# A decoder layer on one core: roots on ScalarE, gain vectors by products, own buffers for the memory's weights, low halves on GpSimd

## The chip, the cores and the metric

The kernel runs on one core of one Trainium2 chip. The metric is the device time of one execution in microseconds (us), less is better. Within a core TensorE multiplies matrices (profile: PE, its weight loads PEld), VectorE (DVE) and ScalarE (ACT) work on tiles, GpSimd (POOL) does the same with other means, and SyncE (SP) here issues nearly all transfers between the chip's main memory and the core's SBUF. [...]

## The reference

One layer over 1024 tokens of 1024 channels, with 256 memory tokens, all in float32:

```
h    = rms_norm(x, norm_mix_pre)                 # x * rsqrt(mean(x*x) + 1e-6) * g
q_d, k_d, v_d, u_p, q_m, gates = split(h @ w_in)
y_attn = diff_attention(q_d, k_d, v_d) @ w_attn_branch      # 8 heads, causal, two softmax maps
y_pool = multiscale_pool(u_p) @ w_pool_branch
mem_n  = rms_norm(mem, norm_mem)
k_m, v_m = split(mem_n @ w_mem_kv)                           # 4 heads of 128
y_mem  = softmax(q_m k_m^T / sqrt(128)) v_m @ w_mem_branch
x  = x + rms_norm((sigmoid-gated sum of y_attn, y_pool, y_mem) @ w_out, norm_mix_post)
h2 = rms_norm(x, norm_ffn_pre)
out = x + rms_norm((gelu(g) * v) @ w_down, norm_ffn_post)    # [g|v] = causal conv3(h2 @ w_up)
```

## The kernel before, in words

Each float32 operand of a product is split in two tiles of a shorter float type: `split` (L82) writes the rounded high half on ScalarE (L86) and the difference, the low half, on VectorE (L87). `mm3` (L94) makes a product of three matmuls: high by high (L95), high by low, low by high (L96, L97).

The change touches three places. The first is the stage that opens the kernel. Rows of 128 tokens of the memory (2 tiles) and of x (8 tiles) are normalized by `norm_rows` (L358): a load per tile (`xt`), the sum of squares by ScalarE's Square with an accumulator (L150; of the memory's second tile on VectorE, L146), the inverse root in `rstd_batch` (L140) by an integer guess and three Newton steps on VectorE (`newton`, L156, twelve short instructions with the scaling of the sum), the scaling of the tile by root and gain in one VectorE instruction (L371), and then `transpose_split` (L170): eight transposes of 128x128 on TensorE (L176), and halves of each four. The gains are loaded as vectors broadcast to all partitions (`load_gain`, L165; tiles gm and gp). Between the pairs of tiles stand the memory's weights: four chunks of 128 key columns and four of 256 rows of value columns, each 512 KB, loaded and split by `wsplit` (L330) through the pool `wst`, in which the raw tile, the high and the low half have two buffers each. A key chunk feeds 24 matmuls of 256 columns (`pk`), a value chunk 12 of 512 columns (`pv`). The first query projection (`pq`, 48 matmuls of 512 columns) and its scores (`pss`) follow.

The second place is the output projection: for each of 8 tiles of tokens two norms by `rstd_of` (L107), one over the product in PSUM, one over the new x, with eleven short VectorE instructions each. The third is the end: `norms` (L1438) takes the roots of four result rows at once while the last but one product runs; the last four rows get half of their sum of squares early (`start_row`, L1461), and behind the last products the other half (L1486), the sum, and the root by `rstd_sums` (L122).

All engines run their instructions in order. The order is made by the language's scheduler out of the order of the text and its own estimates; a tile's buffer is waited for by semaphore. Inverse roots in the attention (L1004) use `newton` and are not changed.

## Time and profile before

| | |
|---|---|
| median of 3 runs | 1747.66 us (1745.94 to 1750.28) |
| the profiled execution | 1744.85 us, its span 1742.8 us |
| TensorE busy | 1711.0 us, 98% of the span |
| VectorE, ScalarE, GpSimd busy | 1272.8, 884.7, 45.4 us |
| moved by transfers | 294.95 MB, mean 169 GB/s |

Times in the rows are in us from the start of the span unless marked ns. A row of a timeline tells start, length, engine, line, operation, tile written and tiles read, their shapes, how many instructions were merged, and in brackets how long the engine had been idle and what released it. Matmuls are pipelined: the distance between two starts tells the pace, the length of one holds its way through the array as well. A busy TensorE is not always one at full pace. The state of a wait is inferred from semaphores.

### The profile page before, as it was taken

Reading aid. Unit: us, or ns where it says so; the run is one execution under the profiler, and the core shown is the slowest. Engines: PE = TensorE matmul, PEld = TensorE weight load, DVE = VectorE, ACT = ScalarE, POOL = GpSimd, SP = SyncE. Lnnn points to the kernel's source line nnn. Section 1 sums busy time; section 2 is a strip of 40 time slices with the busy share of each in tenths; the row PEclk is TensorE's granted clock in tenths of the full one; section 3 lists DMA queues with packets and bytes.
Section 4 is the critical chain, followed back from the end, with each engine's and each line's share of the span. In section 5 each row is a group of like instructions: output and inputs, shape, how many; then the busy total and the mean of one; then the engine's idle time right before and its main releaser. Section 6 shows DMA issues by size and latency. Waiting matters only on the chain.

```text
span 1742.8 us, 22648 instructions
## 1 busy us (share of the span) xinstructions
PE 1711.0 (98%) x8138; PEld 1421.4 (82%) x8138; DVE 1272.8 (73%) x2227; ACT 884.7 (51%) x1551; POOL 45.4 (3%) x103
## 2 busy tenths in 40 slices
PE   6999999999999999999999999999999999999997
PEld 5888888888788888888888888888888888888886
DVE  7775875665675568888866567848888888878476
ACT  6434554444544367777744333645555555543452
POOL 0000000000000011111110000000000000000000
PEclk9999999999999999999999999999999999999999
DMA  7784544354784585765557571473433332583343
GB/s 246 253 315 139 170 156 145 123 170 149 247 243 171 179 240 173 186 169 157 152 178 238 181 229 49 155 236 93 124 112 103 121 97 85 205 290 103 109 147 131
DMA packets 232934, 294.95 MB, mean 169 GB/s; under 512 B 15873, under 2 KB 161526, under 8 KB 230134
## 3 DMA queue, kind: packets, MB, share of 16 engines
q1 hardware_dynamic: 229302, 286.13, 51.6%
q0 software_dynamic: 3520, 7.38, 1.2%
q8 instruction: 64, 1.05, 0.2%
q14 instruction: 48, 0.39, 0.1%
HBM read 201.62 MB, written 85.56 MB: 165 GB/s over the span
## 4 chain that ended last, share of the span: by engine, by line
PE 85%; DVE 7%; DMA 4%; ACT 2%; issue 2%; SPq 0%; DVEq 0%; ACTq 0%
PE pa L95 8%; PE pa L97 8%; PE pa L96 8%; PE pb L95 5%; PE pb L97 5%; PE pb L96 5%; PE pss L900 3%; PE poa L956 2%; PE pe L95 2%; PE pe L97 2%; PE pe L96 2%; PE pya L96 2%; PE pya L95 2%; PE pya L97 2%; PE pd L95 2%; PE pd L97 2%
## 5 line engine op out<-in xcount | busy, mean ns | idle before, releaser
L86 ACT ACTIVATE wpage<-s 128x512 fp32r<-128x512 f32 x136 | 85.2, 627 | 106.9 <-PE pb L97 33.7
L87 DVE TENSOR_TENSOR wpage<-s,wpage 128x512 fp32r<-128x512 f32 x136 | 92.5, 687 | 44.8 <-ACT wpage L86 44.8
L1304 DVE SCALAR_TENSOR_TENSOR cvt<-gv,cols,cvt 128x1023 f32<-128x1023 f32 x88 | 112.4, 1277 | 15.6 <-ACT cvt L1300 15.6
L904 DVE CUSTOM_DVE_ANT_0 z<-pss,hbias 128x256 f32<-128x256 f32 (+7 forms) x128 | 94.4, 752 | 25.7 <-PE pss L900 24.6
L909 ACT ACTIVATE z<-z,mx 128x256 f32<-128x256 f32 (+7 forms) x128 | 98.8, 773 | 20.7 <-DVE mx L904 20.5
L95 PE MATMUL pa<-T,wpage 128*128 128x512 f32 x264 | 102.8, 389 | 0.9 <-DVE gv L252 0.9
L96 PE MATMUL pa<-T,wpage 128*128 128x512 f32 x264 | 102.7, 389 | 0.0
L97 PE MATMUL pa<-T,wpage 128*128 128x512 f32 x264 | 102.7, 389 | 0.0
L900 PE MATMUL pss<-ks,q 128*128 128x512 f32 (+5 forms) x384 | 86.5, 349 | 1.4 <-DVE mx L904 1.4
L86 ACT ACTIVATE page<-blk 128x1024 fp32r<-128x1024 f32 (+1 forms) x42 | 41.4, 988 | 85.8 <-PE pe L96 50.6
L87 DVE TENSOR_TENSOR page<-blk,page 128x1024 fp32r<-128x1024 f32 (+1 forms) x42 | 47.4, 1129 | 38.4 <-ACT page L86 38.4
L900 PEld LDWEIGHTS pss<-ks,q 128*128 128x128 f32 x384 | 62.8, 189 | 11.1 <-DVE mx L904 6.2
L86 ACT ACTIVATE wh<-raw 128x1024 fp32r<-128x1024 f32 (+1 forms) x46 | 41.8, 909 | 57.0 <-issue 16.2
L95 PE MATMUL pd<-page 128*128 128x512 f32 x176 | 68.6, 390 | 1.4 <-ACT row L1414 1.4
L96 PE MATMUL pd<-page 128*128 128x512 f32 x176 | 68.5, 389 | 0.0
L97 PE MATMUL pd<-page 128*128 128x512 f32 x176 | 68.5, 389 | 0.0
L95 PE MATMUL pa<-hT,wpage 128*128 128x512 f32 x168 | 65.5, 390 | 0.0
L97 PE MATMUL pa<-hT,wpage 128*128 128x512 f32 x168 | 65.4, 389 | 0.0
L96 PE MATMUL pa<-hT,wpage 128*128 128x512 f32 x168 | 65.4, 389 | 0.0
L956 PEld LDWEIGHTS poa<-aT,v 128*128 128x128 f32 x480 | 60.6, 190 | 3.0 <-ACT srow L976 1.4
L956 PE MATMUL poa<-aT,v 128*128 128x256 f32 (+1 forms) x480 | 62.4, 280 | 0.0
L87 DVE TENSOR_TENSOR wl<-raw,wh 128x1024 fp32r<-128x1024 f32 (+1 forms) x46 | 47.6, 1034 | 18.1 <-ACT wh L86 18.0
(415 smaller groups left out, 5039.1 us busy)
## 6 DMA issues: line engine op xcount, KB each, us to landing
q<-q_d SPq DMA_DIRECT2D x64, 256.0 KB, 5.3
wd<-in_w_down_dram SPq DMA_DIRECT2D x22, 512.0 KB, 5.7
tw_d<-wd SPq DMA_DIRECT2D x11, 1024.0 KB, 4.6
rawv<-in_w_up_dram SPq DMA_DIRECT2D x22, 512.0 KB, 5.8
rawu<-in_w_up_dram SPq DMA_DIRECT2D x22, 512.0 KB, 3.9
ff_d<-cvt SPq DMA_DIRECT2D x22, 512.0 KB, 4.2
blk<-ff_d SPq DMA_DIRECT2D x20, 512.0 KB, 7.2
br<-tw_d SPq DMA_DIRECT2D x20, 512.0 KB, 3.5
```

What stands on the lines that cost most here:

```text
L86: copy = nc.scalar.activation(out=hi, in_=src, func=AF.Copy)
L87: nc.vector.tensor_tensor(out=lo, in0=src, in1=hi.bitcast(F32), op=ALU.subtract)
L95: nc.tensor.matmul(o, ah, bh, start=first, stop=False, skip_group_check=onto)
L96: nc.tensor.matmul(o, ah, bl, start=False, stop=False, skip_group_check=onto)
L97: return nc.tensor.matmul(o, al, bh, start=False, stop=last, skip_group_check=onto)
L900: last["scores"] = nc.tensor.matmul(pss[:, i * H:i * H + m], q[:, j, c, ts], keys, start=(j == 0), stop=(j == 1))
L904: nc.vector.tensor_tensor_reduce(out=halves(z[:, 0:n]), in0=pss.rearrange("p (a m) -> p a m", a=2)[:, 0:parts, 0:m], in1=halves(biases[h][ ...
L909: nc.scalar.activation(out=z[:, 0:n], in_=z[:, 0:n], func=AF.Exp, scale=-1.0, bias=mx[:, c:c + 1], accum_out=sm if c else sums[:, h, t:t + 1])
L956: nc.tensor.matmul(po[:, qs], (vh, vl)[i][:, k, :], w[j][:, ws], start=(n == 0), stop=(n == len(terms) - 1))
L1304: nc.vector.scalar_tensor_tensor(out=cv[:, sh:], in0=u[:, 0:S - sh], scalar=w, in1=cv[:, sh:], op0=ALU.mult, op1=ALU.add)
```

## The change

Inverse roots: `newton`, `rstd_sums` and the two-halves form of `rstd_of` leave the paths named above. ScalarE takes the square root of the mean, VectorE its reciprocal and one Newton step (`rstd_root`, three or four short instructions; one more makes the scaled mean). The second memory tile's squares go from VectorE to ScalarE. The memory's tiles are normalized one by one, x still in pairs. A one-element square root at the start has ScalarE's table loaded; the exponential of the lambda is ordered behind the stage's last root.

Gains: the two vectors are loaded as two rows of one tile, split, and spread over the partitions by eight matmuls with a 2x128 choice of ones and zeros; the scaling reads them from PSUM. Before these matmuls stand 18 transposes of the identity into a tile that nothing reads, and 9 behind them.

Weights: each of the eight raw chunks has a buffer of its own (the pool `rawm`, in the place of `omh` and `oml`, which are allocated after it). All loads of the stage are issued in one list (`ORDER`), x has six buffers instead of four. The low half of a chunk is made by GpSimd.

The x tiles' place changes too: tiles 0 and 1 follow the first two key chunks instead of standing ahead of them, and each later pair follows a pair of chunks.

```diff
+WARM = 18
+ORDER = "m0 m1 w0 w1 x0 x1 w2 w3 x2 x3 w4 w5 x4 x5 w6 w7 x6 x7".split()
...
+    nc.scalar.activation(out=small.tile([P, 1], F32, tag="sm", name="table"), in_=epsilon, func=AF.Sqrt)
...
+    def rstd_root(y, v, root, t):
+
+        nc.vector.reciprocal(out=y, in_=root)
+        if v.shape[-1] == 1:
+            nc.vector.scalar_tensor_tensor(out=t, in0=y, scalar=v, in1=y, op0=ALU.mult, op1=ALU.mult)
+        else:
+            nc.vector.tensor_tensor(out=t, in0=y, in1=y, op=ALU.mult)
+            nc.vector.tensor_tensor(out=t, in0=t, in1=v, op=ALU.mult)
+        nc.vector.scalar_tensor_tensor(out=y, in0=t, scalar=1.5, in1=y, op0=ALU.add, op1=ALU.mult)
...
+        for j, (src, junk) in enumerate(zip(srcs, junks)):
+            nc.scalar.activation(out=junk, in_=src, func=AF.Square, accum_out=st[:, 0, j:j + 1])
+        roots["last"] = nc.scalar.activation(
+            out=st[:, 3, :], in_=st[:, 0, :], func=AF.Sqrt, scale=1.0 / n, bias=epsilon)
+        nc.vector.tensor_scalar(
+            out=st[:, 1, :], in0=st[:, 0, :], scalar1=-0.5 / n, scalar2=-0.5 * EPS, op0=ALU.mult, op1=ALU.add)
+        rstd_root(st[:, 2, :], st[:, 1, :], st[:, 3, :], st[:, 4, :])
...
-        nc.scalar.activation(out=lame, in_=lame, func=AF.Exp)
+        with tc.issue_after(roots["last"].ins):
+            nc.scalar.activation(out=lame, in_=lame, func=AF.Exp)
...
+            def load_raw(j):
+                w = rawp.tile([P, D], F32, name="rawm%d" % j)
...
+            rows = wst.tile([2, D], F32, tag="raw", name="grows", bufs=2)
+            for j, g in enumerate((norm_mem, norm_mix_pre)):
+                nc.sync.dma_start(out=rows[j:j + 1, :], in_=g[0:1, :])
...
+            def keep(n):
+                for j in range(n):
+                    roots["pe"] = nc.tensor.transpose(idle[:, j % 4, :], ident, ident)
+
+            keep(WARM)
+            rhl = [wst.tile([2, D], F32R, tag=t, name="ghl") for t in ("wh", "wl")]
+            split(*rhl, rows)
+            gains = {}
+            for j, n in enumerate("mx"):
+                gains[n] = bank2(name="gain")
+                for i in range(2):
+                    hs = slice(i * H, (i + 1) * H)
+                    for e in range(2):
+                        with tc.issue_after(roots["pe"].ins):
+                            one = nc.tensor.matmul(gains[n][:, hs], choice[:, j, :], rhl[e][:, hs],
+                                                   start=(e == 0), stop=(e == 1))
+            with tc.issue_after(one.ins):
+                keep(WARM // 2)
...
+            def weights(j, k):
+
+                hi, lo = [wst.tile([P, k, D // k], F32R, tag=t, name=t) for t in ("wh", "wl")]
+                raw = raws[j].rearrange("p (k c) -> p k c", k=k)
+                nc.scalar.activation(out=hi, in_=raw, func=AF.Copy)
+                nc.gpsimd.tensor_tensor(out=lo, in0=raw, in1=hi.bitcast(F32), op=ALU.subtract)
+                return hi, lo
+
+            norm_rows(["m0"])
+            norm_rows(["m1"])
...
+                    norm_rows(["x%d" % i for i in range(j - 1, j + 1)])
...
+                if k2 % 2 == 1:
+                    norm_rows(["x%d" % i for i in range(k2 + 3, k2 + 5)])
...
-        nc.scalar.activation(out=junk, in_=pa[t], func=AF.Square, accum_out=st[:, 9:10])
+        nc.scalar.activation(out=junk, in_=pa[t], func=AF.Square, accum_out=st[:, 3:4])
+        nc.scalar.activation(out=st[:, 4:5], in_=st[:, 3:4], func=AF.Sqrt, scale=1.0 / D, bias=st[:, 1:2])
+        nc.vector.scalar_tensor_tensor(out=st[:, 5:6], in0=st[:, 3:4], scalar=-0.5 / D, in1=st[:, 2:3],
+                                       op0=ALU.mult, op1=ALU.add)
+        r = st[:, 6:7]
+        rstd_root(r, st[:, 5:6], st[:, 4:5], st[:, 7:8])
         nc.vector.tensor_tensor(out=c(1, t, 0), in0=pa[t], in1=gfp[:, 0:H], op=ALU.mult)
-        nc.vector.tensor_tensor(out=st[:, 0:1], in0=st[:, 8:9], in1=st[:, 9:10], op=ALU.add)
-        r = rstd_sums(st)
```

## Rows read from the trace of the kernel before

**Rows 1.** The head of the profile's page: the span, and the busy time of TensorE and ScalarE with its share of the span and the count of instructions.

```profile
span 1742.8 us, 22648 instructions
PE 1711.0 (98%) x8138; PEld 1421.4 (82%) x8138; DVE 1272.8 (73%) x2227; ACT 884.7 (51%) x1551; POOL 45.4 (3%) x103
```

**Rows 2.** The waits of TensorE over the whole span: who waited for whom, us in total, times, the longest.

```profile
PE pt L176 <- DVE xn L371: 10.5, 1, 10.5
...
PE pd L95 <- ACT row L1414: 1.4, 1, 1.4
```

**Rows 3.** The groups of TensorE's matmuls from 0 to 64.65 us: line, tiles, shapes, count | busy us, mean ns of one | idle time before them. Lines L96 and L97 have as many as L95 in pk, pv and pq.

```profile
L176 PE MATMUL pt<-ident,xn 128*128 128x128 f32 x80 | 13.0, 305 | 11.3 <-DVE xn L371 10.5 <-DVE meml L87 0.8
L95 PE MATMUL pk<-memh,wh 128*128 128x256 f32 x32 | 10.1, 314 | 1.2 <-ACT wh L86 0.8 <-ACT memh L86 0.4
...
L95 PE MATMUL pq<-hTh,wh 128*128 128x512 f32 x16 | 6.5, 404 | 0.5 <-DVE vml L87 0.5
...
L95 PE MATMUL pv<-wh,memh 128*128 128x512 f32 x16 | 6.2, 407 | 0.6 <-ACT wh L86 0.6
...
L285 PE MATMUL pc<-ident,rows 48*128 48x48 f32 x4 | 0.4, 231 | 0.0
```

**Rows 4.** The chain of work that ended last, in the stretch from 0 to 110 us: start, us, what.

```profile
53.32 0.87 PE pt L176 x8
```

**Rows 5.** The timeline of TensorE, in three stretches: the first products with the memory's weights, the same two microseconds later, and the end of the first query.

```profile
17.00 0.58 PE L95 MATMUL pk<-memh,wh 128*128 128x256 f32 x1 [0.85 <-ACT wh L86]
...
19.94 0.41 PE L96 MATMUL pk<-meml,wh 128*128 128x256 f32 x1
20.15 0.32 PE L97 MATMUL pk<-memh,wl 128*128 128x256 f32 x1
...
22.02 0.28 PE L96 MATMUL pk<-meml,wh 128*128 128x256 f32 x1
22.14 0.28 PE L97 MATMUL pk<-memh,wl 128*128 128x256 f32 x1
...
63.50 0.39 PE L96 MATMUL pq<-hTl,wh 128*128 128x512 f32 x1
63.73 0.39 PE L97 MATMUL pq<-hTh,wl 128*128 128x512 f32 x1
63.95 0.28 PE L95 MATMUL pss<-kmh,qh 128*128 128x256 f32 x1
```

**Rows 6.** Busy time of the engines in the stretch from 10.47 to 20.15 us, with the count of instructions; the last three columns are the granted clock of TensorE, the share of the transfer engines and GB/s.

```profile
10.47:20.15 9.68, 7.64 (x31) 6.58 (x32) 8.93 (x21) 7.70 (x14) 0.00 (x0) 1.00 0.96 294
```

**Rows 7.** The timeline of SyncE's queue at the start: the loads of the memory's two tiles are issued.

```profile
0.74 0.87 SPq L364 DMA_DIRECT2D xt<-in_mem_dram  x2
```

**Rows 8.** The timeline of ScalarE from 0 to 15 us.

```profile
4.09 1.06 ACT L150 ACTIVATE xn<-xt 128x1024 f32<-128x1024 f32 x1 [2.07 <-DMA xt<-in_mem_dram]
5.05 0.19 ACT L150 ACTIVATION_READ_ACCUMULATOR xn<-xt 128x1 f32 x1
...
13.97 1.06 ACT L86 ACTIVATE wh<-raw 128x1024 fp32r<-128x1024 f32 x1 [0.90 <-DMA raw<-in_w_mem_kv_dram]
```

**Rows 9.** The groups of ScalarE from 0 to 58 us, columns as in rows 3.

```profile
L86 ACT ACTIVATE wh<-raw 128x1024 fp32r<-128x1024 f32 x10 | 10.6, 1059 | 7.4 <-DMA raw<-in_w_mem_kv_dram 6.1 <-DVE lamp L297 1.0 <-PE pk L96 0.2
...
L86 ACT ACTIVATE hTh<-pt 128x512 fp32r<-128x512 f32 x16 | 8.9, 594 | 7.3 <-PE pt L176 7.1
...
L86 ACT ACTIVATE kmh<-pk 128x256 fp32r<-128x256 f32 x4 | 1.5, 375 | 0.2 <-PE pk L97 0.2
...
L86 ACT ACTIVATE vmh<-pv 128x512 fp32r<-128x512 f32 x2 | 1.2, 598 | 0.8 <-PE pv L97 0.8
L300 ACT ACTIVATE lame<-lame 128x2 f32<-128x2 f32 x1 | 0.2, 187 | 0.0
```

**Rows 10.** The timeline of VectorE from 0 to 10 us: the second memory tile's squares, the first and the last of the twelve short instructions, the first scaling.

```profile
5.36 1.22 DVE L146 CUSTOM_DVE_ANT_0 xn<-xt 128x1024 f32<-128x1024 f32 x1 [5.36 <-DMA xt<-in_mem_dram]
...
6.70 0.17 DVE L151 TENSOR_SCALAR sb<-sb 128x2 f32<-128x2 f32 x1
...
8.88 0.16 DVE L163 SCALAR_TENSOR_TENSOR sb<-sb 128x2 f32<-128x2 f32 x1
9.07 1.28 DVE L371 SCALAR_TENSOR_TENSOR xn<-xt,sb,gm 128x1024 f32<-128x1024 f32 x1
```

**Rows 11.** The groups of GpSimd over the whole span: the one that reads and writes a tile of some thousand elements per partition.

```profile
L786 POOL TENSOR_SCALAR_AFFINE_SELECT bias<-bias 128x1152 f32<-128x1152 f32 x1 | 1.6, 1609 | 0.0
```

**Rows 12.** The timeline of ScalarE from 283 to 289 us: one of the five table loads of the span.

```profile
285.72 1.28 ACT L623 ACT_TABLE_LOAD   x1
287.01 1.92 ACT L623 ACTIVATE g<-g 128x2048 f32<-128x2048 f32 x1
```

**Rows 13.** Busy time of TensorE, its weight loads, VectorE, ScalarE and GpSimd in the stretch where the output projection begins and in that of the norms of the first four result rows; last columns as in rows 6.

```profile
1000.00:1040.00 40.00, 39.93 (x178) 32.36 (x177) 24.97 (x65) 14.37 (x22) 0.00 (x0) 1.00 0.84 248
1675.00:1705.00 30.00, 28.62 (x126) 23.40 (x126) 29.32 (x39) 19.48 (x27) 0.00 (x0) 1.00 0.65 225
```

**Rows 14.** The timeline of VectorE behind the last product: the scaling by the gain, the first of the twelve short instructions of the root, the result.

```profile
1735.27 0.69 DVE L1487 TENSOR_TENSOR row<-pd,gfp 128x512 f32<-128x512 f32 x1 [0.65 <-ACT blk L1486]
1735.88 0.15 DVE L1488 TENSOR_TENSOR st<-st 128x1 f32<-128x1 f32 x1
...
1737.96 1.41 DVE L1492 SCALAR_TENSOR_TENSOR row<-row,st,x 128x512 f32<-128x512 f32 x2
```

More of the change, by code (lines that the diff above doesn't have):

```diff
@@ L105, in rsqrt_guess @@
             op0=ALU.mult, op1=ALU.add)
-    def rstd_of(src, junk, n=D):
-        st = small.tile([P, 10], F32, tag="st", name="st")
-        if not isinstance(src, list):
-            nc.scalar.activation(out=junk, in_=src, func=AF.Square, accum_out=st[:, 0:1])
-        else:
-            for j in range(2):
-                hs = slice(j * n // 2, (j + 1) * n // 2)
-                nc.scalar.activation(out=junk[:, hs], in_=src[j], func=AF.Square, accum_out=st[:, 8 + j:9 + j])
-            nc.vector.tensor_tensor(out=st[:, 0:1], in0=st[:, 8:9], in1=st[:, 9:10], op=ALU.add)
-        return rstd_sums(st, n)
@@ L140, in rstd_batch @@
-    def rstd_batch(srcs, junks, n=D, halve=False):
-        m = len(srcs)
-        st = small.tile([P, 4, m], F32, tag="sb%d" % m, name="sb", bufs=2)
-        for j, (src, junk) in enumerate(zip(srcs, junks)):
-            if j % 2 == 1 and halve:
-                nc.vector.tensor_tensor_reduce(
-                    out=junk, in0=src, in1=src, scale=1.0, scalar=0.0, op0=ALU.mult, op1=ALU.add,
-                    accum_out=st[:, 0, j:j + 1])
-            else:
-                nc.scalar.activation(out=junk, in_=src, func=AF.Square, accum_out=st[:, 0, j:j + 1])
-        nc.vector.tensor_scalar(
-            out=st[:, 1, :], in0=st[:, 0, :], scalar1=64.0 / n, scalar2=64.0 * EPS, op0=ALU.mult, op1=ALU.add)
-        newton(st[:, 2, :], st[:, 1, :], st[:, 3, :])
-        return [st[:, 2, j:j + 1] for j in range(m)]
+    epsilon = const.tile([P, 1], F32, name="epsilon")
@@ new lines, with rstd_batch @@
+    roots = {}
+    def rstd_batch(srcs, junks, n=D):
+        m = len(srcs)
+        st = small.tile([P, 5, m], F32, tag="sb%d" % m, name="sb", bufs={1: 4, 2: 2, 4: 1}[m])
+        for j, (src, junk) in enumerate(zip(srcs, junks)):
[5 more added lines that the diff above has]
+        rstd_root(st[:, 2, :], st[:, 1, :], st[:, 3, :], st[:, 4, :])
+        return [st[:, 2, j:j + 1] for j in range(m)]
@@ new lines, in load_rows @@
+            def load_rows(src, i):
+                xt = pa.tile([P, D], F32, tag="xt", name="xt", bufs=6)
+                nc.sync.dma_start(out=xt, in_=src[i * P:(i + 1) * P, :])
+                return xt
+            def load_raw(j):
+                w = rawp.tile([P, D], F32, name="rawm%d" % j)
+                if j < MH:
+                    nc.sync.dma_start(out=w.rearrange("p (k c) -> p k c", c=P), in_=chunk(w_mem_kv, j * P))
+                else:
+                    r = (j - MH) * 2 * P
+                    nc.sync.dma_start(out=w.rearrange("p (k c) -> p k c", c=H),
+                                      in_=w_mem_kv[r:r + 2 * P, H:2 * H].rearrange("(k p) c -> p k c", p=P))
+                return w
@@ new lines @@
+            choice = pa.tile([2, 2, P], F32R, name="choice", bufs=1)
+            nc.vector.tensor_copy(out=choice, in_=pick)
+            idle = bank((P, 4, P), "idle")
+            def keep(n):
[13 more added lines that the diff above has]
+                                                   start=(e == 0), stop=(e == 1))
@@ new lines, with norm_rows @@
+            with tc.issue_after(one.ins):
+                keep(WARM // 2)
+            raws, xts = [], {}
+            for what in ORDER:
+                if what[0] == "w":
+                    raws.append(load_raw(int(what[1])))
+                else:
+                    xts[what] = load_rows(mem if what[0] == "m" else x, int(what[1]))
+            def norm_rows(names):
+                srcs = [xts.pop(n) for n in names]
+                xns = [pa.tile([P, D], F32, tag="xn", name="xn", bufs=4) for _ in names]
+                rs = rstd_batch(srcs, xns)
+                for n, xt, xn, r in zip(names, srcs, xns, rs):
+                    i = int(n[1])
+                    hi, lo = (memh, meml) if n[0] == "m" else (hTh[i // 4], hTl[i // 4])
+                    nc.vector.scalar_tensor_tensor(
+                        out=xn, in0=xt, scalar=r, in1=gains[n[0]],
+                        op0=ALU.mult, op1=ALU.mult)
+                    transpose_split(xn, hi, lo, i % 4 * P)
@@ L406 @@
             make_lambda(kvp)
+        ostack = ExitStack()
+        opool = ostack.enter_context(tc.tile_pool(name="omT", reuse_waits="tile", bufs=1, side="left"))
+        omh = [opool.tile([P, S], F32R, name="omh%d" % j) for j in range(MH)]
+        oml = [opool.tile([P, S], F32R, name="oml%d" % j) for j in range(MH)]
         mscale = float(P) ** -0.5
```

62 lines of the change are left out of this document (14 added, 48 removed).

## The prediction

> **What bounds the kernel now.** I read the page's head first [rows 1]: TensorE is busy 1711.0 of 1742.8 us, ScalarE 51%. Only work that ends TensorE's waiting, lets it run faster, or shortens what lies ahead of its first or behind its last product can move the end. Then TensorE's waits [rows 2]: one of 10.5 us before the first transpose, everything else 1.4 us or less. So the change can act at the start, in the stage that normalizes the memory and x, and at the end.
>
> How much the start costs, I get by counting. At 63.95 us the first scores begin; the stage and the first query are done by then. TensorE's work up to there [rows 3], at the spacing it has when it runs freely: 80 transposes at 0.87/8 us [rows 4], 8.7; 96 products of 256 columns at 0.115 [rows 5], 11.0; 48 + 48 of 512 columns at 0.23 [rows 5], 22.1; four transposes of the columns, 0.4. Together 42.2 us in 63.95, so 21.8 us are lost:
> - 10.5 until the first transpose.
> - From 10.47 to 20.15 us: 9.7 us for 16 transposes and 15 small products, which are 3.5 us of work, so 6.2 lost. [...]
> - After 20.15: 5.1, small waits for weights' halves and for transfers (ScalarE alone waits 6.1 us for weights [rows 9]).
>
> **The change part by part.**
> *Start.* SyncE issues the two gain rows first, two issues of some 0.43 us each [rows 7], so the first rows of the memory arrive 0.85 us later. Before, they were there at 4.09, the second at 5.36, and the first weights, the seventh half-megabyte, at 13.97 [rows 8, 10]: 1.64 us for each in a row of transfers. The two broadcast gains (1 MB) fall out of that row. In the new order: m0 4.9, m1 6.2, w0 7.8, w1 9.5, x0 11.1, x1 12.8, and so on to x7 at 32.4. No later transfer waits for the kernel: the weights have own buffers, and x4, which reuses m0's, is issued long after m0 is used. What waits behind x4 on SyncE (w6, w7, the rest of x) is needed much later.
>
> m1 is the row that decides. It no longer shares VectorE's twelve short steps with m0 (6.70 to 9.07 [rows 10]). Square and its sum, 1.2 [rows 8], to 7.4; a root on ScalarE like the short exponential, 0.19 [rows 9], to 7.6; reciprocal and two steps at 0.2, to 8.3; scaling 1.28 [rows 10], to 9.6; eight transposes, about 0.9, and the two halves of the last four, 0.6 on ScalarE [rows 9] and 0.7 on VectorE (128x512 out of PSUM, as in [rows 14]): some 11.8. With 0.2 for the hops that is 12.0. The gain can be later: if its rows take as long from issue as the first memory tile (0.74 to 4.09), the second lands at 4.5, its halves (1.06 and 1.2) are there at 6.8, the last three of the memory gain's products, 0.43 each at the slow pace, at 8.1, and m0 and m1 are scaled one after the other until 10.7: the start is at 13.1. If so small a transfer takes a microsecond and a half less, nothing is late. I take the middle, 12.5, for the first product with the weights, where it ran in earnest at 17.0 before [rows 5]. Sixteen transposes (1.7) are done by then, so 10.8 us are lost, not 16.7.
>
> *Clock.* 18 dummy transposes from about 2 us on, eight gain products and nine more transposes keep TensorE at work ahead of m0. Before, the pace rose after 9.7 us of work with gaps; now such work begins 10 us ahead of the weights' products, so I count these at 0.115. The nine transposes and x's gain products (2.0 and 1.7 us at the slow pace, half at the other) lie between the memory's gain and its scaled rows, which are 1.3 us apart or more: no further charge.
>
> *Low halves on GpSimd.* No row shows a subtraction there. The nearest is a select over 128x1152, 1.61 us [rows 11], one tensor read: 1.43 for 1024. Twice that, 2.9, is the other bound, as two are read. I take 2.2, midway, as neither end has the nearer row. A page's buffers serve every second page: high half 1.06, low half 2.2, products 24 x 0.115 = 2.75 make 6.0 us in a cycle of two pages, in which TensorE has two pages and two rows of x, 7.2. So GpSimd holds on average, but the second page of a pair, with no transposes ahead of it, comes 0.5 us late plus hops: with six such pages some 2 us. VectorE loses eight halves of 1.2 us and most short steps, and is no limit.
>
> [...]
>
> *ScalarE.* It takes the second memory row's square and all roots. After 12.5 us it has eight squares at 1.15, sixteen halves at 0.53, six pages at 0.96, key and value halves 2.2, roots 0.8 (lengths of [rows 9], as starts lie some 0.1 closer than lengths): 26.5 us, against 29.0 for TensorE (11.0 + 11.0 + 64 transposes). That leaves little slack, so I count 3 us of stalls after 12.5, where 5.1 came before; bounds are 1 and 6.
>
> *Tables.* Three switches come new: to the exponential at the lambda, to the root ahead of the output projection, and to it again after the channel mixer. A switch takes 1.28 us, and the next instruction follows at once [rows 12]: 3.9 us of ScalarE, the first in the busy stage (in the 3 us), the others where TensorE is busy 39.9 of 40 us and ScalarE half idle [rows 13]. [...]
>
> *Output projection and row norms.* Shorter chains for sixteen norms there, but TensorE does not wait: nothing. In the norms of the first four result rows VectorE loses some 1.5 us and ScalarE gains as much; TensorE is idle 1.4 of 30 us [rows 13]: nothing, within 1 either way.
>
> *End.* After the last product: the last square, then on VectorE from 1735.27 the scaling by the gain and twelve short steps until 1737.96 [rows 14]. Left are that 0.61, two steps at 0.25 and two at 0.2, 1.5 to 1.75 with the root on ScalarE (0.19) beside them: 1.1 saved.
>
> *Sum.* 21.8 - (10.8 + 3.0) = 8.0, and 1.1: **9.1 us**. Behind the stage TensorE's waits are few and short [rows 2], so what is won at the start reaches the end; the next late thing is ScalarE's queue. The profiled execution took 1744.85 us (span 1742.8); it lies 2.8 under the median of 1747.66. Taken off the median: **1738.6 us**.
>
> **The rivals.**
> *A, GpSimd and VectorE get in each other's way.* [...] Chance 0.14.
>
> *B, ScalarE or a cold TensorE takes the gain.* ScalarE is 91% filled with all ten squares in order with pages; with the order unlucky, 4 us more are lost. [...] Chance 0.13.
>
> *C, GpSimd becomes the bound (slower).* Its first subtraction starts at 8.9 and the last page's products follow the eighth; before, the same work, the query's 48 products and the columns taken out, ended at 63.95 - 11.4 = 52.5. With 8.9 + 8P + 2.75 = 52.5 + 1.1 it decides from P = 5.2 us; below it slower pages only eat gain. At 7 us it ends at 67.7: 15 - 1 = 14 us slower, 1762. Against it: the select at 1.61 for 1152 elements would have to be a poor guide by a factor of four. Chance 0.07.
>
> **How the numbers follow.** Forecast 0.66, with its own range 1733 to 1742.4 (stalls of 1 to 6 us, the 1 us of the norms, a median that moves by 2); A 0.14; B 0.13; C 0.07. A measurement of this kernel tells 0.3%, 5.2 us, from no change, so faster means under 1742.4: all of the forecast, a third to a half of A and B, 0.77. The rest of A and B is within 0.3%, 0.16; C is slower, 0.07. The range goes from 1733 to 1745.5: it takes in A and B, leaves out C and some of the forecast's and A's ends.
>
> **What would show it.** In the profile after: the first scaled row near 7 to 8.5 us and products with the weights from 12.5, 0.115 us apart; eight GpSimd subtractions near 2.2 us; the first scores starting near 56 where it was 63.95; three table loads more; the last scaling 1.5 to 1.8 us after the last square. Wrong would be: subtractions over 3 us, TensorE's waits for low halves or for the transposes' copies summing to more than 6 us, weights landing later than 1.64 us apart, or spacings of 0.21 beyond 12.5 us.

## The result, and the profile after

The change made the kernel slower: 1754.51 us median of 7 runs (1752.11 to 1759.03) against 1746.48 us of the kernel before on the same chip (7 runs, 1744.4 to 1750.28), a ratio of 1.0043, 95% interval 1.0029 to 1.0057. That is 8 us more, where 9.1 less were forecast, and outside the range. A second measurement, with other runs of both, gave 1.0042 (1.0027 to 1.0056). The profiled execution took 1756.1 us; it is 11.3 us over the profiled one of before, of which some 3 us are the two runs' own (below).

The head of the page of the changed kernel, in answer to [rows 1]: TensorE has 14 us more of busy time, VectorE 20 us less.

```profile
span 1754.1 us, 22570 instructions
PE 1725.1 (98%) x8173; PEld 1430.3 (82%) x8173; DVE 1252.3 (71%) x2044; ACT 896.6 (51%) x1585; POOL 65.1 (4%) x114
```

TensorE's waits in the changed kernel from 0 to 75 us, in answer to [rows 2]: who waited for whom, us in total, times, the longest. The wait of 10.5 us ahead of the first transpose is no longer there, as other work now stands ahead of it; that transpose starts at 9.88 us instead of 10.47. But three waits of some 3 us are new.

```profile
PE pt L162 <- DVE hTl L89: 3.0, 1, 3.0
PE pt L162 <- DVE meml L89: 2.9, 1, 2.9
PE pv L97 <- DVE kml L89: 2.8, 1, 2.8
PE idle L374 <- POOL ident masks.py:199: 1.7, 1, 1.7
PE gain L386 <- DVE sb L116: 0.6, 1, 0.6
```

The timeline of TensorE of the changed kernel, in answer to [rows 5]: the idle transposes (L374), the norm vectors' products (L386), m0's and m1's transposes, the first product of the keys, its pace three microseconds later, and the first scores.

```profile
1.71 4.10 PE L374 MATMUL idle<-ident 128*128 128x128 f32 x18 [1.71 <-POOL ident masks.py:199]
6.44 2.09 PE L386 MATMUL gain<-ghl,choice 2*128 2x512 f32 x8 [0.64 <-DVE sb L116]
8.46 1.62 PE L374 MATMUL idle<-ident 128*128 128x128 f32 x9
9.88 1.92 PE L162 MATMUL pt<-ident,xn 128*128 128x128 f32 x8
14.66 1.25 PE L162 MATMUL pt<-ident,xn 128*128 128x128 f32 x8 [2.87 <-DVE meml L89]
16.01 0.80 PE L97 MATMUL pk<-memh,wh 128*128 128x256 f32 x2
...
18.82 0.41 PE L98 MATMUL pk<-meml,wh 128*128 128x256 f32 x1
19.04 0.41 PE L99 MATMUL pk<-memh,wl 128*128 128x256 f32 x1
...
19.42 0.27 PE L98 MATMUL pk<-meml,wh 128*128 128x256 f32 x1
19.53 0.28 PE L99 MATMUL pk<-memh,wl 128*128 128x256 f32 x1
...
68.01 0.28 PE L97 MATMUL pss<-kmh,qh 128*128 128x256 f32 x1
```

The keys' first product starts at 16.01, not at 12.5, and the products then start some 0.21 us apart until 19.25, not 0.115. The first scores start at 68.01, which is 4.06 us later than before [rows 5]. Behind the stage the loss goes on growing: the last product starts 13.1 us later than before (1747.21 against 1734.07), and the shorter tail gives 1.4 us of it back. Of the 13.1 us, 1.0 arises at TensorE's wait for a row from ScalarE ahead of the last products: 2.4 us where it was 1.4 [rows 2], and 2.0 to 2.5 in the profiles of e2, e9 and the changed kernel again. What causes that was not tested.

The timeline of VectorE in the changed kernel, where the root of a pair of x tiles is worked out, first of x0 and x1, then of x2 and x3:

```profile
17.27 0.15 DVE L120 TENSOR_TENSOR sb<-sb 128x2 f32<-128x2 f32 x1
17.45 0.16 DVE L121 TENSOR_TENSOR sb<-sb 128x2 f32<-128x2 f32 x1
...
22.47 0.17 DVE L116 RECIPROCAL sb<-sb 128x2 f32<-128x2 f32 x1 [0.71 <-ACT sb L132]
22.67 2.07 DVE L120 TENSOR_TENSOR sb<-sb 128x2 f32<-128x2 f32 x1
24.77 2.35 DVE L121 TENSOR_TENSOR sb<-sb 128x2 f32<-128x2 f32 x1
27.15 0.16 DVE L122 SCALAR_TENSOR_TENSOR sb<-sb 128x2 f32<-128x2 f32 x1
```

And GpSimd's timeline in the same kernel, with two subtractions merged in the row:

```profile
22.33 4.77 POOL L415 TENSOR_TENSOR wl<-rawm,wh 128x1024 fp32r<-128x1024 f32 x2 [6.49 <-ACT wh L414]
```

The same two steps on two elements a partition take 0.15 us at 17.27 and 2.07 and 2.35 us at 22.67. The subtractions run from 22.33 to 27.10; each step ends when one of them ends. At 35.32 and 37.42 us it happens again (2.06 and 2.31 us). That is rival A: the two engines get in each other's way. In these rows the subtraction came first each time.

The timeline of ScalarE in the changed kernel:

```profile
8.25 1.06 ACT L414 ACTIVATE wh<-rawm 128x1024 fp32r<-128x1024 f32 x1 [0.58 <-DMA rawm<-in_w_mem_kv_dram]
11.31 1.06 ACT L131 ACTIVATE xn<-xt 128x1024 f32<-128x1024 f32 x1 [1.99 <-DMA xt<-in_x_dram]
12.27 0.19 ACT L131 ACTIVATION_READ_ACCUMULATOR xn<-xt 128x1 f32 x1
12.36 1.04 ACT L414 ACTIVATE wh<-rawm 128x1024 fp32r<-128x1024 f32 x1
13.31 1.06 ACT L88 ACTIVATE memh<-pt 128x512 fp32r<-128x512 f32 x2
```

m0's transposes are done at 11.8, but their high halves (L88) stand in ScalarE's queue behind the square of x0, which waits 1.99 us for its load, and behind the second weight. So m1's transposes, which need m0's buffers in PSUM (the memory that this kernel's products are written to), start 2.87 us late.

### The profile page after: what moved, and what is told of

Its sections match the earlier page's. It is cut to its first block, busy times and chain, and to the rows that moved or that the text cites. A ratio compares the mean times of both kernels' runs of the same rounds, so it can differ in the third digit from the quotient of the medians.

```text
span 1754.1 us, 22570 instructions
## 1 busy us (share of the span) xinstructions
PE 1725.1 (98%) x8173; PEld 1430.3 (82%) x8173; DVE 1252.3 (71%) x2044; ACT 896.6 (51%) x1585; POOL 65.1 (4%) x114
## 4 chain that ended last, share of the span: by engine, by line
PE 75%; issue 13%; DMA 5%; DVE 3%; POOL 2%; ACT 2%; SPq 0%; POOLq 0%; DVEq 0%; ACTq 0%
PE pa L97 8%; PE pa L99 8%; PE pa L98 8%; PE pb L98 5%; PE pb L97 5%; PE pb L99 5%; PE pd L97 2%; PE pd L99 2%; PE pd L98 2%; PE pe L97 2%; PE pe L99 2%; PE pe L98 2%; PE pout L98 1%; PE pout L99 1%; PE pout L97 1%
## 5 line engine op out<-in xcount | busy, mean ns | idle before, releaser
L88 ACT ACTIVATE wpage<-s 128x512 fp32r<-128x512 f32 x136 | 85.3, 627 | 107.3 <-DVE s L180 43.8
L97 PE MATMUL pa<-T,wpage 128*128 128x512 f32 x264 | 102.9, 390 | 0.8 <-DVE gv L238 0.8
L88 ACT ACTIVATE page<-blk 128x1024 fp32r<-128x1024 f32 (+1 forms) x42 | 41.3, 988 | 92.7 <-PE pe L98 50.6
L97 PE MATMUL pd<-page 128*128 128x512 f32 x176 | 68.6, 390 | 2.4 <-ACT row L1456 2.4
L97 PE MATMUL pa<-hT,wpage 128*128 128x512 f32 x168 | 65.5, 390 | 0.0
L99 PE MATMUL pa<-hT,wpage 128*128 128x512 f32 x168 | 65.4, 389 | 0.0
L98 PE MATMUL pa<-hT,wpage 128*128 128x512 f32 x168 | 65.4, 389 | 0.0
L97 PEld LDWEIGHTS pa<-T,wpage 128*128 128x128 f32 x264 | 49.6, 188 | 11.9 <-DVE gv L238 1.2
L88 ACT ACTIVATE wh<-raw 128x1024 fp32r<-128x1024 f32 (+1 forms) x38 | 33.4, 878 | 50.4 <-issue 16.5
```

The source lines that it names most:

```text
L88: copy = nc.scalar.activation(out=hi, in_=src, func=AF.Copy)
L97: nc.tensor.matmul(o, ah, bh, start=first, stop=False, skip_group_check=onto)
L98: nc.tensor.matmul(o, ah, bl, start=False, stop=False, skip_group_check=onto)
L99: return nc.tensor.matmul(o, al, bh, start=False, stop=last, skip_group_check=onto)
```

## The experiments

Each experiment was timed beside the kernel before on one chip, in five rounds. The ratio is to the kernel before; mean clock is the mean of the granted clock over all timed executions (0.998 for the kernel before). The two times are of one profiled execution each. The experiments come in four groups, each on its own chip (e1 to e4; e5 to e8; the changed kernel again with e9, e10 and e12; e14 and e15), so ratios of two groups are compared by way of the kernel before.

| run | ratio, 95% interval | first keys' product, first scores (us) | mean clock |
|---|---|---|---|
| changed kernel | 1.0043 (1.0029 to 1.0057) | 16.01, 68.01 | 0.995 |
| again | 1.0042 (1.0027 to 1.0056) | 16.42, 69.5 | 0.994 |
| e1, low halves on VectorE | 1.0011 (1.0002 to 1.0020) | 16.73, 63.3 | 0.996 |
| e2, root steps with one input | 1.0001 (0.9990 to 1.0012) | 16.68, 61.52 | 0.997 |
| e3, copies first | 1.0022 (1.0013 to 1.0031) | 16.03, 67.2 | 0.997 |
| e4, kernel before, shifted | 1.0015 (1.0005 to 1.0025) | 15.10, 64.6 | 0.998 |
| e5, old addresses | 1.0013 (1.0000 to 1.0025) | 17.05, 66.9 | 0.995 |
| e6, e2 and old addresses | 0.9974 (0.9964 to 0.9985) | 16.48, 61.4 | 0.996 |
| e7, all mended | 0.9967 (0.9953 to 0.9981) | 15.46, 60.5 | 0.997 |
| e8, e6 without idle transposes | 0.9964 (0.9950 to 0.9978) | 14.78, 58.1 | 0.998 |
| e9, e7 without idle transposes | 0.9959 (0.9945 to 0.9973) | 14.17, 59.00 | 0.999 |
| e10, changed kernel without them | 1.0007 (0.9997 to 1.0018) | 14.63, 62.7 | 0.997 |
| e12, e9 with VectorE's low halves | 1.0010 (0.9998 to 1.0021) | 14.6, 65.98 | 0.997 |
| e14, ScalarE's order | 1.0023 (1.0012 to 1.0034) | 15.00, 65.0 | 0.997 |
| e15, e14 without idle transposes | 1.0006 (0.9995 to 1.0018) | 14.63, 65.4 | 0.998 |

Theory: GpSimd's subtractions stall VectorE's small root steps. Rivals: ScalarE's order and late transfers hold the stage; the addresses that the change moves slow products far behind it; the clock.

**e1: the low halves back on VectorE.**

```diff
-                nc.gpsimd.tensor_tensor(out=lo, in0=raw, in1=hi.bitcast(F32), op=ALU.subtract)
+                nc.vector.tensor_tensor(out=lo, in0=raw, in1=hi.bitcast(F32), op=ALU.subtract)
```

> One part undone: VectorE makes the low halves of the memory's weights again; the ScalarE roots, the norm vectors by products and the own buffers stay. In the changed kernel two steps of the root of a pair of x tiles took 2.07 and 2.35 us instead of 0.15 to 0.16 us, just while two subtractions of GpSimd ran back to back, and TensorE then waited 3.0 and 2.8 us. The contention theory (a VectorE step with two operands in SBUF stands still while GpSimd's subtraction runs): with nothing large on GpSimd every such step takes 0.15 to 0.25 us; VectorE takes over 8 subtractions of about 1.2 us, 9.8 us in all, of which much lies beside products; the first scores come 3 to 5 us before those of the changed kernel (68.0 us), at 63 to 65 us, and the total is 2 to 6 us under the changed kernel's, within 0.3% of the kernel before. The rival (the order of ScalarE's work and the late transfers hold the stage, GpSimd does nothing): the steps may shrink, but the first scores stay at 67 to 69 us, or come later by what VectorE takes over.

First scores at 63.3 us, 4.7 before the changed kernel's, and 0.32% off the ratio (5.6 us), both as the contention theory had it. TensorE's longest wait behind the start is 1.0 us. It doesn't tell stalled steps from GpSimd's length, though: both went. e2 does, which leaves GpSimd its subtractions.

**e2: the same subtractions, but root steps that read one tensor.**

```diff
+        elif v.shape[-1] == 2:
+            for j in range(2):
+                c = slice(j, j + 1)
+                nc.vector.tensor_scalar(out=t[:, c], in0=y[:, c], scalar1=y[:, c], scalar2=v[:, c],
+                                        op0=ALU.mult, op1=ALU.mult)
+            for j in range(2):
+                c = slice(j, j + 1)
+                nc.vector.tensor_scalar(out=y[:, c], in0=t[:, c], scalar1=1.5, scalar2=y[:, c],
+                                        op0=ALU.add, op1=ALU.mult)
+            return
```

> GpSimd keeps the subtractions; the root of a pair of x tiles is worked column by column, each step with one operand of two dimensions in SBUF and the others as scalars of a partition (four steps in place of three). The contention theory in its narrow form (only steps that read two tensors from SBUF stand still): no step of the root takes over 0.4 us beside GpSimd's subtractions; the waits of TensorE of 3.0 and 2.8 us go, the granted clock no longer falls to half at 29.6 us, the first scores come at 60 to 63 us instead of 68.0, and the total is 5 to 8 us under the changed kernel's, that is within 0.3% of the kernel before. In a wide form (every VectorE step that reads SBUF stands still) the steps still take about 2 us, and the time is that of the changed kernel within 2 us. The rival without contention: the first scores stay at 67 to 69 us.

VectorE's timeline in this run:

```profile
22.34 0.17 DVE L116 RECIPROCAL sb<-sb 128x2 f32<-128x2 f32 x1 [0.70 <-ACT sb L142]
22.54 0.46 DVE L122 TENSOR_SCALAR sb<-sb 128x1 f32<-128x1 f32 x2
22.91 0.33 DVE L126 TENSOR_SCALAR sb<-sb 128x1 f32<-128x1 f32 x2
```

GpSimd's in the same run:

```profile
22.20 2.40 POOL L425 TENSOR_TENSOR wl<-rawm,wh 128x1024 fp32r<-128x1024 f32 x1 [6.15 <-ACT wh L424]
```

The steps run through beside a subtraction of full length: 0.20 to 0.27 us each. TensorE's waits of 3.0 and 2.8 us for the x tiles and the keys are gone; the one ahead of m1's transposes stays (2.0 us here), as ScalarE's order does. In this profile the granted clock no longer falls at 30 us (1.00 from 29 to 34 us, where the changed kernel has 0.63 from 30 to 34), the first scores are 6.5 us earlier, and the ratio falls by 0.42%: 7.3 us for four stalled steps of 2.06 to 2.35 us. So the narrow form of the theory holds. The mean clock rose as well, from 0.995 to 0.997; what part of the 7.3 us is the clock's, these runs do not separate.

**e3: m0's and m1's copies first on ScalarE.** The copies' last instruction is kept in `held`; the second weight and the squares of x0 and x1 are issued behind it.

```diff
+                with tc.issue_after(held[0].ins) if held and names[0] in ("x0",) else nullcontext():
+                    rs = rstd_batch(srcs, xns)
...
+                with tc.issue_after(held[0].ins) if j == 1 else nullcontext():
+                    nc.scalar.activation(out=hi, in_=raw, func=AF.Copy)
```

> ScalarE's order changed: the copies of the high halves of m0 and m1 come before the second weight's high half and before the squares of x0 and x1, which wait for x0's load. The theory that ScalarE's order holds the first products: the first product of the memory's keys starts at 13 to 13.5 us instead of 16.0, the first scores 2 to 4 us before 68.0, and the total falls by as much. The contention theory alone: the two waits of 3.0 and 2.8 us for the slowed roots stay, since GpSimd's subtractions still meet them, and the first scores come at most 1 us earlier, as what is gained ahead of the roots is waited for at them.

The total fell by 0.21% (3.7 us), as much as the order's theory has it, but the first product stayed at 16.03 and the first scores came only 0.8 us earlier, as the contention theory alone has it. In this profile the norm vectors' products ran at the lower pace (3.75 us instead of 2.09), so m0's transposes began at 12.21 instead of 9.88; from there to the first product it took 3.8 us instead of 6.1. So this run does not show where its 3.7 us come from, and the order is priced by e14. Nor are its stalled steps those of the changed kernel: two of the four stayed (1.67 and 1.90 us), and another kind showed, a step with one tensor and two constants on 128x2. VectorE:

```profile
40.80 2.01 DVE L134 TENSOR_SCALAR sb<-sb 128x2 f32<-128x2 f32 x1
42.73 0.15 DVE L116 RECIPROCAL sb<-sb 128x2 f32<-128x2 f32 x1
```

GpSimd, same run:

```profile
40.40 4.74 POOL L420 TENSOR_TENSOR wl<-rawm,wh 128x1024 fp32r<-128x1024 f32 x2 [4.70 <-ACT wh L419]
```

**e4 and e5: addresses.** The change's new small buffers put every later tile of SBUF's left side 192 bytes further; tiles of the right side stay. e5 takes the shift out of the changed kernel, and e4 gives it to the kernel before:

```diff
+    nc.gpsimd.memset(const.tile([P, 48], F32, name="shift"), 0.0)
```

e5, with the square root's small constant in a tile of the right side, and fewer buffers for the small ones:

```diff
...
-    epsilon = const.tile([P, 1], F32, name="epsilon")
+    epsilon = pad8[:, 0:1]
...
-        st = small.tile([P, 5, m], F32, tag="sb%d" % m, name="sb", bufs={1: 4, 2: 2, 4: 1}[m])
+        st = small.tile([P, 5, m], F32, tag="sb%d" % m, name="sb", bufs={1: 3, 2: 2, 4: 1}[m])
...
-        st = small.tile([P, 10], F32, tag="st", name="st")
+        st = small.tile([P, 10], F32, tag="st", name="st", bufs=4)
```

> The kernel before with one unused constant of 192 bytes a partition, cleared once by GpSimd, which puts every later tile of the left side of SBUF 192 bytes further, where the changed kernel has them; nothing else differs. The address theory (products that read one operand from the left side and one from the right are paced by where these lie): the spacing of the matmuls of pya goes from 0.2265 to 0.2308 us to about 0.2327, those of pb and pout rise likewise, and the total is 2 to 4 us over the kernel before. The rival (the change's later losses come from its start, through the order of loads and the granted clock): spacings as in the kernel before, and a time within 1 us of it.

> The changed kernel with the 192 bytes taken back out of the small buffers, so that every later tile of the left side of SBUF lies where it lay in the kernel before; the memory's weights, roots and GpSimd's subtractions stay. The address theory, after the run that shifted the kernel before by 192 bytes and gave a ratio of 1.0015 with pya's spacing at 0.2320 to 0.2327 us: the spacings go back to 0.2265 to 0.2308 us, and the ratio to the kernel before falls from 1.0043 to about 1.0025 (3 us). The rival (the later loss of the changed kernel is the granted clock's and the loads'): spacings may go back, but the ratio stays at 1.0035 to 1.0045. Either way the contended root steps of about 2 us stay.

Mean distance of two starts (us), worked out over all matmuls of the kind that follow each other without a gap:

| product, matmuls | before | e4, shifted | changed kernel | e5, shift taken out |
|---|---|---|---|---|
| pb, low half of ypl by wh, 64 | 0.2258 | 0.2329 | 0.2329 | 0.2261 |
| pya, high by low, 128 | 0.2265 | 0.2320 | 0.2327 | 0.2293 |
| pya, all three, 384 | 0.2289 | 0.2324 | 0.2325 | 0.2289 |
| pout, low by high, 127 | 0.2276 | 0.2298 | 0.2305 | 0.2276 |
| pa, of a page and hT, 503 | 0.2268 | 0.2269 | 0.2268 | 0.2268 |

The rows of pya's second group show it without any working: first and last start. The kernel before:

```profile
L96 PE MATMUL pya<-atl,wh x128: 388/394/501, 919.4 to 1006.9; 128*128 128x512 f32 x128
```

The changed kernel:

```profile
L98 PE MATMUL pya<-atl,wh x128: 387/393/504, 928.3 to 1017.3; 128*128 128x512 f32 x128
```

The changed kernel with the shift taken out:

```profile
L98 PE MATMUL pya<-atl,wh x128: 388/388/397, 925.0 to 1012.3; 128*128 128x512 f32 x128
```

It is 87.5, 89.0 and 87.3 us for the same work. The products in the table with one operand on either side change with the shift, and as a whole change back; those with both on the left (a page and hT) don't. Over all products the distances sum up to 3.6 us in the changed kernel and 3.2 in e4, where the ratio says 2.6. e5's ratio fell by 0.30% (5.2 us), more than the 3 expected. The two intervals leave room for that, and its profile has three stalled steps where the changed kernel has four, so the 5.2 us need not all be the addresses'.

**e6: e2 and the old addresses together.**

> The run with the root of a pair worked column by column (ratio 1.0001) and the old addresses besides. If contention and addresses are separate and add up: first scores at 61 to 62 us, pya's spacings at 0.2265 to 0.2308 us, and a ratio of 0.998 to 0.9985, which is 2.5 to 3.5 us under the kernel before. If they don't add up (the first run's gain was the granted clock's luck, or the start's gain is waited for later): a ratio of 0.9995 to 1.0005.

0.9974, 4.7 us below e2, and a little under the range expected: the two add up, and the kernel is faster than before.

**e10, e8: without the idle transposes.** WARM = 1 leaves one of them ahead of the norm vectors and none behind.

```diff
-WARM = 18
+WARM = 1
```

> The changed kernel with one idle transpose in place of 18 and none in place of 9 behind the norm vectors' products; all else stays, the contended root steps and the addresses too (the planner moves some steps of the start, since fewer instructions are ahead of them). The theory that the dummies don't buy the clock, but cost some: 1 to 3 us less than the changed kernel, ratio 1.0025 to 1.004, a mean granted clock nearer to the kernel before. The prediction's step (the dummies buy the pace of the first products): 1.5 to 4 us more than the changed kernel, ratio 1.005 to 1.0065.

> As the run with the pair's root column by column and the old addresses, but with one idle transpose ahead of the norm vectors' products in place of 18, and none behind them in place of 9. The theory that the dummies buy the clock (the prediction's step: the first product of the keys at 0.115 us spacing): without them the granted clock is at half in the first 20 us, the keys' first products are 0.21 us apart up to about 20 us, and first scores come 1.5 to 3 us later. The rival (the breaks between dummies, norm vectors and products make the clock fall again, so that the dummies bring nothing): half speed lasts as long with them as without, and the first scores differ by less than 1 us; the first transposes even come up to 1 us earlier, as no idle transposes stand ahead of them.

Both came out against the prediction: without the transposes that were to buy the pace, the changed kernel became 6.1 us shorter (1.0042 to 1.0007, below the ranges of both theories), and the first keys' product came at 14.63. e8 is 0.10% below e6, within the two intervals. Busy time of the engines in stretches of the changed kernel; the last three columns are granted clock, share of the transfer engines, GB/s:

```profile
8.00:12.00 4.00, 3.79 (x20) 3.02 (x18) 2.67 (x4) 1.76 (x2) 2.36 (x1) 0.64 1.07 364
12.00:16.00 4.00, 1.25 (x8) 0.84 (x8) 1.73 (x4) 4.00 (x9) 2.37 (x1) 0.93 1.15 314
16.00:20.00 4.00, 3.99 (x19) 3.77 (x20) 3.90 (x8) 2.93 (x6) 0.00 (x0) 0.58 1.03 397
...
30.00:34.00 4.00, 4.00 (x24) 4.00 (x23) 2.91 (x6) 2.55 (x6) 0.00 (x0) 0.63 0.10 24
```

The same of e10:

```profile
8.00:12.00 4.00, 4.00 (x14) 2.87 (x12) 2.85 (x4) 2.66 (x3) 2.39 (x2) 1.00 1.07 358
12.00:16.00 4.00, 3.44 (x15) 2.58 (x14) 2.25 (x4) 3.70 (x9) 2.31 (x1) 1.00 1.15 317
16.00:20.00 4.00, 4.00 (x33) 4.00 (x33) 3.72 (x7) 1.34 (x4) 0.00 (x0) 1.00 1.02 393
```

In the changed kernel the granted clock reads 0.58 to 0.64 in three of these windows, and 0.50 in single microseconds of them (10 to 12, 16 to 19, 30 to 33); in the same windows of e10 it reads 1.00. That is no rule: e7, with the idle transposes, reads 1.00 throughout the first 64 us, and e15, without them, reads 0.88 from 30 to 34 and 0.96 from 34 to 64. But e10 differs in another thing: the planner ordered ScalarE anew, with the second weight at 10.27 and m0's copies at 11.45, ahead of x0's square, and e8 in the same way. The stalls of e10 differ too; one is of a third kind, a step with one scalar and two tensors:

```profile
28.33 2.26 DVE L122 SCALAR_TENSOR_TENSOR sb<-sb 128x2 f32<-128x2 f32 x1
```

GpSimd, same run:

```profile
28.20 2.38 POOL L415 TENSOR_TENSOR wl<-rawm,wh 128x1024 fp32r<-128x1024 f32 x1 [1.20 <-ACT wh L414]
```

e14 and e15 part the order from the idle transposes.

**e14, e15: one order of ScalarE, with and without idle transposes.** As e3, but only the squares of x0 and x1 are held, not the second weight:

```diff
-                with tc.issue_after(held[0].ins) if j == 1 else nullcontext():
-                    nc.scalar.activation(out=hi, in_=raw, func=AF.Copy)
+                roots["w%d" % j] = nc.scalar.activation(out=hi, in_=raw, func=AF.Copy)
```

> The changed kernel with its idle transposes, addresses and root steps as they are, and one rule for ScalarE: the squares of x0 and x1 come after the four copies of the high halves of m0 and m1 (the second weight may come ahead of these, as it did in the run without idle transposes, where ScalarE no longer stood 2.0 us for x0's load and TensorE waited 0.6 us instead of 2.7 for m0's copies). If it was this order that the run without idle transposes gained by (1.0007 against 1.0042): first product of the keys at 14 to 15 us, ratio 1.0005 to 1.0015. If the idle transposes themselves cost the time, by a granted clock that falls to half in the first 34 us: the granted clock falls here too, and the ratio is 1.0025 to 1.004.

> The same rule for ScalarE, without the idle transposes, so that ScalarE's work up to the first product of the keys has the same order as in the run beside it. If the order alone was the gain: within 0.0007 of the run beside it. If the idle transposes cost by themselves: 0.0015 to 0.003 below the run beside it, with a granted clock of 1.00 through the first 34 us and a mean granted clock of 0.997 to 0.998 instead of 0.994 to 0.996.

The order alone gives 1.0023, 0.19% (3.3 us) below the changed kernel; that lies between the two expectations, the intervals of the two kernels meet, and the first scores come 3.1 us earlier. Taking the idle transposes out gives 0.17% more (1.0006), though these intervals meet too and the first scores do not come earlier (65.42 against 64.95 us). The pair e7 and e9, below, gives 0.08%. So no gain by the transposes is seen in any pair; a cost of up to 3 us is likely, but no pair with ScalarE in one order shows it clear of noise. How they can cost, the mended kernel (e7) shows in TensorE's timeline:

```profile
5.73 3.78 PE L401 MATMUL gain<-ghl,choice 2*128 2x512 f32 x8
9.44 2.18 PE L387 MATMUL idle<-ident 128*128 128x128 f32 x9
11.42 1.92 PE L174 MATMUL pt<-ident,xn 128*128 128x128 f32 x8
```

m0 was scaled from 8.44 to 9.7 us, but nine idle transposes at the lower pace (2.18 us, where the changed kernel has 1.62) stand ahead of its own until 11.42. In e9 the norm vectors' products start at 3.76 and m0's transposes at 9.84. Nor do they buy the pace: the count of the keys' products ahead of the first two that follow at 0.12 us is 14, 13, 19, 5, 2, 17, 6, 2 and 6 in the nine profiles with idle transposes (the changed kernel, again, e1, e2, e3, e5, e6, e7, e14) and 3, 9, 7, 6 and 21 in the five without (e8, e9, e10, e12, e15). The idle transposes don't sort them; what does stays open.

**e7, e9: all mended, with and without idle transposes.** Column-wise root steps (also L134), old addresses, e3's order, and the cast of the choice matrix ahead of the norm rows' low halves on VectorE, where it had stood behind m0's square:

```diff
+            cast = nc.vector.tensor_copy(out=choice, in_=pick)
...
+            with tc.issue_after(cast.ins):
+                roots["rows"] = nc.vector.tensor_tensor(out=rhl[1], in0=rows, in1=rhl[0].bitcast(F32), op=ALU.subtract)
```

> All that the runs so far point to in one kernel: pairs' roots column by column (also the step with two constants, which took 2.01 us beside a subtraction in one run), the old addresses, ScalarE's copies of m0 and m1 ahead of the second weight and of the squares of x0 and x1, and VectorE's cast of the selecting matrix ahead of the low halves of the norm rows, so that the norm vectors' products start when the dummies end (5.8 us in place of 6.4). If ScalarE's order is worth what the transposes waited (2.3 to 2.9 us) and the rest adds up: first product of the keys at 12.5 to 14 us, first scores at 57 to 60 us, ratio 0.996 to 0.9975. If the order brings nothing, as its first run had it: first product at 15.5 to 16.5 us, first scores at 61 to 62 us, ratio 0.998 to 0.9985.

The ratio, 0.9967, is in the range expected for an order that counts; the first product (15.46) and the first scores (60.5) are later than expected, as the nine idle transposes stand ahead of m0's.

> The kernel with all that was mended (0.9967), without the dummies. If the dummies' loss and the mends are separate: the norm vectors' products start at 5.0 us instead of 5.8, first scores at 56 to 58 us, ratio 0.995 to 0.9965. If what the run without dummies gained (0.9964 against 0.9974) was the changed order of the start, that the mended kernel has in another way: ratio 0.9965 to 0.9975.

e9 is the fastest kernel of the study: 1742.15 us median where the kernel before has 1747.76 (0.9959). Its ratio is in the range expected; its first scores, 59.00, are later than the 56 to 58. Its first keys' product, 14.17, is still 1.7 us behind the forecast.

**e12: e9 with the low halves on VectorE.**

> The same kernel with the low halves of the memory's weights on VectorE, which tells whether GpSimd's part of the change is worth anything once it meets no step that it stalls. VectorE takes over 8 subtractions of 1.2 us. If VectorE is near its limit in the stage of the weights and the x tiles (8 us of 9 busy in some stretches), first scores come 2 to 4 us later than with GpSimd, ratio 0.9975 to 0.9985. If VectorE has room, the difference is under 1 us, since its subtraction ends 1.2 us earlier than GpSimd's 2.4.

1.0010 against 0.9959, first scores 65.98 against 59.00: GpSimd's subtractions are worth some 8 us where they meet no step that they stall, twice what was expected. VectorE is busy 27.15 of 30 us between 34 and 64. And e12 is no faster than e1 (1.0010, 1.0011), though it has the order and the addresses mended and no idle transposes besides. With the low halves on VectorE these three brought nothing in sum, so the prices below hold for the kernel with GpSimd's subtractions and not for any other.

**The changed kernel again.**

> The changed kernel once more, unedited, on the chip of the three runs beside it. All theories: a ratio of 1.003 to 1.0055. A second profile tells what of the later loss belongs to the kernel: the two stalled root steps and the spacings of pya (0.232 to 0.233 us) must come again; the fall of the granted clock at 449 us, which the first profile had with its 2.5 us, comes again only if the kernel makes it, and else was that run's own.

The waits (3.1, 2.8, 2.7 us) and pya's distances (0.2330 to 0.2338) came again. The fall of the clock at 449 us (0.61 from 449 to 451 and 0.54 from 451 to 453 in the first profile, where it was put at some 2.5 us) did not: it reads 1.00 from 440 to 460 here. It was that run's own.

## Why the prediction was wrong, step by step

- *"VectorE loses eight halves of 1.2 us and most short steps, and is no limit."* This is the step that failed most. It is no limit by busy time, but two root steps in two pairs stood still for nearly a whole subtraction each. In the sum the term is the stalls after the first product, 3.0 us with bounds of 1 and 6. By the prediction's own count of TensorE's work (42.2 less 1.7) they were 11.5 us, from 16.01 to 68.01; in e2, without the four stalled steps, 4.3. Rival A, that GpSimd and VectorE get in each other's way, had this with a chance of 0.14. It was two stalls in each of two norms, 8.8 us, of which the first scores saw 6.5, and the granted clock read 0.50 from 30 to 33 us, behind TensorE's break of 3.0: 7.3 us in all (e2). m1's root is done before the first subtraction starts at 9.40, but x's roots come later.
- *First product of the keys at 12.5 us.* It was 16.01. The arrivals were right (m0's square near 4.9, w0's high half at 8.25), m0 was scaled at 8.23; but ScalarE's queue put x0's square, with its load at 11.3, ahead of m0's copies. Rival B named an unlucky order, at 4 us; e14 prices it at 3.3 us.
- *"so I count these at 0.115"* and *"no further charge"* for the nine transposes. Both wrong. The first 14 products ran mostly 0.21 us apart, other profiles have 2 to 21 such products with the idle transposes or without, and the nine stand in the way of m0's. Price: 0 to 3 us.
- *Addresses.* No step had them. 3 to 5 us (2.6 by e4, 4.7 by e6 against e2, 5.2 by e5), nearly all of it behind the stage, where the prediction said that what is won or lost at the start reaches the end unchanged.
- *GpSimd's subtraction 2.2 us*: right, 2.39 mean of eight. Rival C is out.
- *Tables*: three more loads of 1.28 us, as forecast. Beside none of them does TensorE stand idle for more than 0.13 us.
- *End, 1.1 us*: right side, mis-sized. From the start of the last square to the start of the last result it is 2.04 us (1747.63 to 1749.67) instead of 3.41: 1.4 us. For the row norms *"nothing, within 1 either way"* was forecast; TensorE's wait ahead of the last products grew by 1.0 us, so that 0.4 of it is left at the end.
- *Sum.* What was taken off one at a time, 7.3 for the stalls, 3.3 for the order, 3 to 5 for the addresses and 0 to 3 for the idle transposes, is 14 to 19 us; all at once, from 1.0043 to 0.9959, it is 15 us. Without these four the change brings 0.41%, 7 us of the 9.1 that were forecast (e9 has one more edit, the earlier cast); its first scores come 5.0 us earlier than before, where 8.0 were forecast. So the account of the gains had the right size and was somewhat too high, and the account of what the change costs missed two terms, the addresses and the idle transposes, and had two, the stalls and the order, among its rivals and not in its sum. The ends that the range has for A and B were the author's estimates, and no run shows them; the runs show 7.3 us for the stalls and 3.3 for the order. That the four prices add up is shown for this set alone (see e12).

Whether the idle transposes' cost is the queue's or the clock's stays open, and so does why the shift by 192 bytes changes a product's pace.

## What to carry to other kernels

When work goes to GpSimd, go through the small instructions of VectorE that run beside it, not its busy time: in these runs one that reads two tensors from SBUF (1.67 to 2.35 us instead of 0.15), or (in one form, on 128x2) one tensor with two constants (2.01 us), waited for the end of the GpSimd subtraction that ran; rewritten column by column it took 0.20 to 0.27 us for each column instead of some 2. Look at what stands in a queue ahead of the instruction that frees a buffer, and whether that has its data: m0's copies stood behind a square that waited 1.99 us for its load. And compare the distances of products that the edit doesn't touch: here new small buffers moved every later tile on one side of SBUF by 192 bytes, and 0.2258 us became 0.2329.

## What the runs showed of the hardware

- A VectorE step of 0.15 us took 2.07 and 2.35 us beside GpSimd's subtraction; one with a scalar and two tensors took 2.26 us (e10), and one with one tensor and two constants on 128x2 took 2.01 us (e3). Not slowed were steps on 128x1 with scalars of a partition (0.20 to 0.27 us), the reciprocal on 128x2 (0.17 us at 22.47), and a scaling with the gain in PSUM (2.47 us for two at 23.71 in e3, with a subtraction from 24.61).
- A shift of 192 bytes of the operands on one side of SBUF changed the distance of 512-column products by up to 3% (0.2258 to 0.2329 us), and back (0.2261).
- The pace of the first products is not read off the granted clock alone: in e10 it reads 1.00 from 8 to 20 us, and the products are 0.21 us apart until 16.4, as in the kernel before until 20.15 [rows 5, 6].
